# Making twelve weight remainders with an accumulating transfer in place of a VectorE subtraction

## The chip, the cores and the metric

The kernel runs on one core of one Trainium2 chip. The metric is device time in microseconds (us) for one execution, taken as the median of several runs; lower is better. Beside the times there is a profile of one execution: for each engine of the core (TensorE for matrix products, VectorE and ScalarE for work on elements, GpSimd and SyncE, which here mostly issue transfers) when each instruction ran, and for the transfers when they were issued and landed.

## The reference

The reference is a decoder trunk of two layers over 512 tokens of width 1024, in float32. Each layer is a half-step SwiGLU feed-forward, a mixer, and a second half-step SwiGLU. The change is in the mixer, whose first step is one projection of the normalised input:

```python
h = rms_norm(x, mix_norm[l]) @ w_mix_in[l]
(c_x, c_b, c_c, h_q, h_f, h_i, h_g, f_q, f_k, f_v, f_f) = jnp.split(h, split_at, axis=-1)
y = jnp.concatenate([short_conv_mixer(...), hgrn2_mixer(h_q, h_f, h_i, h_g, ...), fox_mixer(...)], axis=-1)
x = x + y @ w_mix_out[l]
```

`h_f`, `h_g` and `h_q` are 256 columns each: the forget logits, the gate and the query of a gated linear recurrence (HGRN2). The products must be close to float32 exact.

## The kernel before

**Products in three parts.** TensorE takes float32 operands at full rate in a rounded form, fp32r. To keep the accuracy, each operand is split in two: `hi`, the value rounded to fp32r, and `lo`, the remainder `src - hi`. A product is then three: hi x hi, hi x lo and lo x hi, all accumulated in one PSUM bank. This is `mm3` (lines 321 to 339); its three matmuls stand in the profile as L328, L336 and L337. Where weights are the first operand, as in the streams below, L328 and L336 read the weight's `hi`, and L337 reads its `lo`.

**Granules.** Weights come from DRAM in granules of two blocks of 128 rows. `granule` (lines 289 to 304) loads one into a tile `st` of 128 partitions by up to 1024 elements (two buffers) on the sync queue (L297), and calls `parted` (lines 306 to 319). That makes a tile `hl` (three buffers) that holds `hi` in its first and `lo` in its second half: a cast on ScalarE (L314), then a subtraction on VectorE (L315). `st` can be loaded again when both have read it; `hl` when the granule's last matmul has read it.

**Streams.** `stream_steps` (lines 345 to 382) walks over the eight blocks of 128 rows (KD = 8) in four granules, k = 0, 2, 4 and 6, and issues their matmuls. For 256 columns there are two jobs, one for each 128 columns with a bank of its own; a granule is 2 blocks x 2 jobs x 3 products = 12 matmuls that move 512 tokens each. The remainder of a granule is first read by its third matmul. The last granule of a stream goes job by job, the others block by block.

**The start of the mixer.** In `mix` (from line 1030) three such streams follow each other: `bz` (forget logits, L1092), `bg` (gate, L1093) and `bq` (query, L1116). They begin while the feed-forward before them ends: its last granules and the norm's sums are still on the engines. Before the last granule of `bz`, `norm` closes the root mean square (L447, and the activations at L277). Then comes a stream with 264 columns that uses tokens as the first operand (L1122), and the recurrence starts. GpSimd's queue holds a memset, a copy and eight small loads of constants at the mixer's beginning (L1043 to L1055); their tiles lie where tiles of the feed-forward were, and so they wait for its last instructions. Between the mixers GpSimd issues the accumulating transfers of the feed-forward (L786, L827).

**What sets the order.** The program is traced in the order of the code. The framework then places each instruction on its engine by readiness in its own estimate and by priority, gives out tile buffers, and adds the semaphores; on the chip every engine runs its own list in order. The work of `parted` stands in a block of high priority when the granule is made ahead, as it is in these three streams. `follow` fixes the order by hand in the feed-forward, not here.

The functions that the diff touches:

Of the kernel before, what the change touches and what calls it, by code (L numbers as in the profile page):

```python
# [9 lines left out]
F32 = mybir.dt.float32  # L10
F32R = mybir.dt.float32r
# [3 lines left out]
AF = mybir.ActivationFunctionType  # L15
ALU = mybir.AluOpType
# [8 lines left out]
P = 128  # L25
# [3 lines left out]
KD = D // P  # L29
# [22 lines left out]
C_X, C_B, C_C, H_Q, H_F, H_I, H_G = (256 * i for i in range(7))  # L52
# [107 lines left out]
class Trunk:  # L160
# [115 lines left out]
    def act(self, out, in_, func, **kw):  # L276
        i = self.nc.scalar.activation(out, in_, func, **kw)  # L277
        if self.tab is not None:
            self.tc.add_manual_dep(i.ins, self.tab, NOSYNC, reason="table order")
        self.tab_users.append(i.ins.name)  # L280
        return i
# [4 lines left out]
        self.chain[engine] = i.ins.name  # L286


    def granule(self, parts, kk, ahead=True, skew=0, keep=False, queued=False, first=False):
        nc = self.nc  # L290
        c = sum(ap.shape[1] for ap in parts)
        st = self.wp.tile([P, 1024], F32, tag="st", name=self.n("st"), bufs=2)
        s3 = st[:, : kk * c].rearrange("p (k c) -> p k c", k=kk)
        at = 0
        for ap in parts:
            w = ap.shape[1]
            d = nc.sync.dma_start(s3[:, :, at : at + w], ap.rearrange("(k p) c -> p k c", p=P))  # L297
            if queued:
                self.follow("s", d)
            at += w  # L300
        with self.tc.high_priority() if ahead and not keep else ExitStack():
            hi, lo = self.parted(st[:, : kk * c], 1 if ahead else kk, skew, keep or first)
        h3, l3 = (a.rearrange("p (k c) -> p k c", k=kk) for a in (hi, lo))
        return [(h3[:, i, :], l3[:, i, :]) for i in range(kk)]

    def parted(self, src, pieces=1, skew=0, keep=False):
        nc = self.nc
        n = src.shape[1]
        hl = self.wp.tile([P, 2 * 1024 + 64], F32R, tag="hl", name=self.n("hl"), bufs=3)
        hh, ll = (hl[:, a + skew : a + skew + n] for a in (0, 1024))  # L310
        w = n // pieces
        for c in range(0, n, w):
            hi, lo = hh[:, c : c + w], ll[:, c : c + w]
            a = nc.scalar.copy(hi, src[:, c : c + w])  # L314
            b = nc.vector.tensor_sub(lo, src[:, c : c + w], hi)  # L315
            if pieces > 1 or keep:
                self.follow("a", a)
                self.follow("v", b)
        return hh, ll
# [22 lines left out]
        for _ in self.stream_steps(*args, **kw):  # L342
            pass

    def stream_steps(self, jobs, parts_of, act, nk, mid=None, pre=None, given=None, queued=False, ending=None, calm=False):
        k = 0
        while k < nk:
            kk = min(2, nk - k)
            if callable(mid) and k == nk - 2:
                mid()  # L350
            if pre is not None:
                pre(k)
            end = k + kk == nk
            if end and ending is not None:
                jobs = ending
            skew = SKEW_MOVING if jobs[0][2] is not None and jobs[-1][0].shape[-1] < T else 0
            keep = given is not None and given(k)
            rows = self.granule(
                parts_of(k, kk), kk, pre is None and not (calm and k == 0), skew, keep,
                queued, queued and k == 0,  # L360
            )
            if keep:
                yield
            order = (
                [(job, j) for job in jobs for j in range(kk)]
                if end
                else [(job, j) for j in range(kk) for job in jobs]
            )
            for n, ((acc, cols, toks, *more), j) in enumerate(order):
                if pre is not None and n == len(order) // 2:  # L370
                    pre(k, True)
                if isinstance(mid, tuple) and (k, len(order) // 2) == (mid[0], n):
                    mid[1]()
                ah, al = act(k + j)
                hi, lo = rows[j]
                first, last = k + j == 0 and not more, end and j == kk - 1
                if toks is None:
                    self.mm3(acc, hi[:, cols], lo[:, cols], ah, al, first, last)
                else:
                    self.mm3(acc, ah[:, toks], al[:, toks], hi[:, cols], lo[:, cols], first, last)  # L380
            k += kk
            yield
# [647 lines left out]
    def mix(self, l, w, w_out, conv_w, out_gain, q_gain, k_gain, f_bias, next_gain):  # L1030
        nc, tc = self.nc, self.tc
        FM2 = [slice(0, P), slice(P, 2 * P)]
        TOK = [slice(c, c + P) for c in (0, 128, 256, 384)]
        with tc.tile_pool(name=self.n("mix"), bufs=1) as mp:
# [23 lines left out]
            def cols(*spans):  # L1058
                return lambda k, kk: [w[k * P : (k + kk) * P, a : a + n] for a, n in spans]

            def features_steps(spans, banks, mid=None):
                bs = [self.bank(t) for t in banks]
                yield from self.stream_steps(
                    [(b, c, None) for b, c in zip(bs, FM2)], cols(*spans), self.xact, KD, mid
                )
                return bs

            def features(*args):
                g = features_steps(*args)
                while True:  # L1070
                    try:
                        next(g)
                    except StopIteration as e:
                        return e.value

            def tokens(a, banks=("mm", "mm")):
# [12 lines left out]
            norm = lambda: self.end_norm(  # L1089
                self.bank("pt"), hp, self.parted_norm(hp, (self.tt,) * 2, self.tb)  # L1090
            )
            bz = features([(H_F, 256)], ("mm", "mm"), norm)  # L1092
            bg = features([(H_G, 256)], ("mm", "po"))  # L1093
            inv = self.inv
            z, q = (hp.tile([P, 2, T], F32, tag=t, name=self.n(t)) for t in ("z", "q"))
            sg = hb.tile([P, 2, T], F32, tag="sg", name=self.n("sg"))
# [16 lines left out]
                out=self.inv2, in0=self.invc, scalar=1.0 / HD, in1=self.invc,  # L1113
                op0=ALU.mult, op1=ALU.mult,
            )
            bq = features([(H_Q, 256)], ("mm", "mm"))  # L1116

            for i in range(2):
                nc.vector.tensor_mul(q[:, i, :], bq[i], inv)
# [64 lines left out]
            def conv():  # L1184
                for i in range(2):
                    bx, bc = yield from features_steps(
                        [(C_X + i * P, P), (C_C + i * P, P)], ("mm", "mm")
                    )
                    if i == 0:
                        inv2 = ap2.tile([P, T], F32, tag="t", name=self.n("iv2"), bufs=self.tb)  # L1190
                        nc.scalar.activation(inv2, inv, AF.Square)
                    self.conv_in(ap2, i, bx, bc, inv2, cw)
                bb = yield from features_steps([(C_B, 256)], ("mm", "mm"))
                for i in range(2):
                    self.conv_out(ap2, i, bb[i])
# [43 lines left out]
            for dg in range(2):  # L1239
                banks = self.next4()  # L1240
# [676 lines left out]
```

## Time and profile before

| | |
|---|---|
| median of 3 runs | 1803.4 us (1801.94 to 1804.28) |
| span of the profiled execution, first to last instruction | 1799.0 us |
| time of the profiled execution itself | not given apart from its span; the runs are 2.9 to 5.3 us above the span |
| TensorE busy | 1791.7 us, 14271 matmuls |
| VectorE busy | 1441.6 us, 2022 instructions |
| ScalarE busy | 993.2 us, 1429 instructions |
| GpSimd busy | 176.9 us, 184 instructions |
| the three streams, first mixer | 336.9 to 370.0 us of the span |
| the three streams, second mixer | about 889.9 us later |

In the lines that follow, a group reads: source line, engine, operation, the tile written and the tiles read, partitions x elements and type, count, then busy time in us and the mean of one in ns, and the idle time of the engine before these instructions with what ended it. In a timeline a line begins with the start and the duration in us. PE is TensorE, DVE is VectorE, ACT is ScalarE, POOL is GpSimd, SP is SyncE; a q behind the name is the engine's queue of issued work. Matmul durations are modelled and overlap; what counts is the distance from one start to the next.

### The profile page before, as it was taken

How to read it: one execution, taken by the hardware profiler on the slowest of the kernel's cores; microseconds unless marked ns; L12 is line 12 of the kernel's file. 1: busy time of each engine (PE TensorE's matmuls, PEld its weight loads, DVE VectorE, ACT ScalarE, POOL GpSimd, SP SyncE). 2: the span in 40 equal slices, each digit the busy share in tenths (PEclk: the TensorE clock that was granted, in tenths of full speed). 3: DMA queues.
4: the chain of work that ended last, by engine and by line, in shares of the span. 5: the costliest groups of instructions: out<-in, count | busy, mean ns of one | idle time of the engine just before them, and what ended most of it. 6: DMA issues, size and time to landing. Idle time of an engine off the chain costs nothing.

```text
span 1799.0 us, 34748 instructions
## 1 busy us (share of the span) xinstructions
PE 1791.7 (100%) x14271; PEld 1681.2 (93%) x14271; DVE 1441.6 (80%) x2022; ACT 993.2 (55%) x1429; POOL 176.9 (10%) x184
## 2 busy tenths in 40 slices
PE   9999999999999999999999999999999999999999
PEld 7899999899888899999889999998998888999997
DVE  9888887776888798879679887876868879888893
ACT  6455554464776464556446555555547755555551
POOL 0011120100000002112001111201000000020210
PEclk9999999999999999999999999999999999999999
DMA  7668783233433857868275787813234346686762
GB/s 209 178 144 184 180 180 96 71 81 84 106 103 104 228 136 160 194 162 165 82 208 132 170 187 187 172 65 83 78 86 115 89 143 180 165 163 189 161 133 94
DMA packets 244638, 254.09 MB, mean 141 GB/s; under 512 B 18904, under 2 KB 228576, under 8 KB 244480
## 3 DMA queue, kind: packets, MB, share of 16 engines
q1 hardware_dynamic: 189424, 182.38, 33.3%
q0 software_dynamic: 54752, 69.23, 23.8%
q8 instruction: 112, 1.84, 0.4%
q14 instruction: 46, 0.38, 0.1%
q10 hardware_dynamic: 304, 0.27, 0.1%
HBM read 223.98 MB, written 2.10 MB: 126 GB/s over the span
## 4 chain that ended last, share of the span: by engine, by line
PE 96%; DVE 2%; ACT 1%; DMA 0%; issue 0%; SPq 0%; ACTq 0%; DVEq 0%
PE mm L328 14%; PE mm L336 14%; PE mm L337 14%; PE sc L328 7%; PE sc L336 7%; PE sc L337 7%; PE pt L328 6%; PE pt L336 6%; PE pt L337 6%; PE po L328 4%; PE po L336 4%; PE po L337 4%; PE po L1648 1%; PE pt L1692 1%; PE sc L1841 1%; PE pt L1841 1%
## 5 line engine op out<-in xcount | busy, mean ns | idle before, releaser
L810 ACT CAST hl<-w 128x1024 fp32r<-128x1024 f32 x322 | 336.9, 1050 | 312.1 <-PE mm L337 82.7
L812 DVE TENSOR_TENSOR hl<-w,hl 128x1024 fp32r<-128x1024 f32 x322 | 392.4, 1222 | 80.4 <-ACT hl L810 80.4
L315 DVE TENSOR_TENSOR hl<-st,hl 128x512 fp32r<-128x512 f32 (+3 forms) x196 | 162.7, 831 | 115.6 <-ACT hl L314 114.5
L314 ACT CAST hl<-st 128x512 fp32r<-128x512 f32 (+3 forms) x196 | 143.1, 732 | 173.7 <-PE po L337 67.8
L328 PE MATMUL mm<-xc,hl 128*128 128x256 f32 (+1 forms) x733 | 201.2, 276 | 0.0
L336 PE MATMUL mm<-xc,hl 128*128 128x256 f32 x728 | 201.2, 276 | 0.0
L337 PE MATMUL mm<-xc,hl 128*128 128x256 f32 x728 | 201.0, 276 | 0.0
L328 PE MATMUL sc<-xc,hl 128*128 128x256 f32 (+1 forms) x532 | 146.0, 276 | 0.0
L336 PE MATMUL sc<-xc,hl 128*128 128x256 f32 x528 | 146.0, 276 | 0.0
L337 PE MATMUL sc<-xc,hl 128*128 128x256 f32 x528 | 145.8, 276 | 0.0
L328 PEld LDWEIGHTS mm<-xc,hl 128*128 128x128 f32 x733 | 137.4, 188 | 0.2
L336 PEld LDWEIGHTS mm<-xc,hl 128*128 128x128 f32 x728 | 136.7, 188 | 0.0
L337 PEld LDWEIGHTS mm<-xc,hl 128*128 128x128 f32 x728 | 136.7, 188 | 0.0
L328 PE MATMUL pt<-xc,hl 128*128 128x256 f32 (+1 forms) x482 | 132.6, 276 | 0.0
L336 PE MATMUL pt<-xc,hl 128*128 128x256 f32 x480 | 132.6, 276 | 0.0
L337 PE MATMUL pt<-xc,hl 128*128 128x256 f32 x480 | 132.5, 276 | 0.0
L328 PE MATMUL mm<-x,hl 128*128 128x512 f32 x272 | 107.6, 396 | 0.0
L336 PE MATMUL mm<-x,hl 128*128 128x512 f32 x272 | 106.3, 391 | 0.0
L337 PE MATMUL mm<-x,hl 128*128 128x512 f32 x272 | 106.2, 390 | 0.0
L328 PEld LDWEIGHTS sc<-xc,hl 128*128 128x128 f32 x532 | 99.7, 188 | 0.2
L336 PEld LDWEIGHTS sc<-xc,hl 128*128 128x128 f32 x528 | 99.1, 188 | 0.0
L337 PEld LDWEIGHTS sc<-xc,hl 128*128 128x128 f32 x528 | 99.1, 188 | 0.0
(512 smaller groups left out, 5579.6 us busy)
## 6 DMA issues: line engine op xcount, KB each, us to landing
w<-in_ffn_w_in_dram SPq DMA_DIRECT2D x140, 512.0 KB, 5.6
w<-in_ffn_w_out_dram SPq DMA_DIRECT2D x64, 512.0 KB, 4.6
w<-in_ffn_w_out_dram POOLq DMA_DIRECT2D x56, 512.0 KB, 8.2
st<-in_w_mix_in_dram SPq DMA_DIRECT2D x88, 256.0 KB, 2.7
st<-in_ffn_w_in_dram SPq DMA_DIRECT2D x70, 256.0 KB, 2.9
w<-in_ffn_w_in_dram POOLq DMA_DIRECT2D x35, 512.0 KB, 8.5
w<-S POOLq DMA_DIRECT2D x35, 512.0 KB, 4.8
st<-in_ffn_w_out_dram SPq DMA_DIRECT2D x24, 512.0 KB, 6.0
```

Of the source, the lines that this page charges most:

```text
L314: a = nc.scalar.copy(hi, src[:, c : c + w])
L315: b = nc.vector.tensor_sub(lo, src[:, c : c + w], hi)
L328: i = nc.tensor.matmul(acc[:, c], ah, bh[:, c], start=first and c.start == 0, stop=False, skip_group_check=True,)
L336: nc.tensor.matmul(acc, a, b, start=False, stop=False, skip_group_check=True)
L337: i = nc.tensor.matmul(acc, c, d, start=False, stop=last, skip_group_check=True)
L810: A(nc.scalar.copy(hi, src))
L812: return lambda: V(nc.vector.tensor_sub(lo, src, hi))
L1648: nc.tensor.matmul(self.ob[:, t0 + u * P : t0 + 2 * P], V[:, j, h % 4].rearrange("p a d -> p (a d)"), part[:, j, u:, :].rearrange("p i t - ...
L1692: nc.tensor.transpose(tb[:, j * P : (j + 1) * P], p[:, j * P : (j + 1) * P], self.ident)
L1841: E(nc.tensor.matmul(acc, wh[j][l][:, cols], (self.xh, self.xl)[r][k + j], start=k + j == 0 and which == 0, stop=k + j == KD - 1 and which ...
```

## The change

For six granules in each mixer, those with k = 2 and k = 6 of the three streams `bz`, `bg` and `bq`, the remainder is made in another way. ScalarE first writes the negated rounded value into `lo`. GpSimd then issues a transfer from `st` to `lo` that adds, which leaves `src - hi` there. ScalarE makes `hi` with a second cast, as before. VectorE has no part in these granules. The other granules, and all other streams, stay as they were.

```diff
-    def granule(self, parts, kk, ahead=True, skew=0, keep=False, queued=False, first=False):
+    def granule(self, parts, kk, ahead=True, skew=0, keep=False, queued=False, first=False, adding=False):
...
         with self.tc.high_priority() if ahead and not keep else ExitStack():
-            hi, lo = self.parted(st[:, : kk * c], 1 if ahead else kk, skew, keep or first)
+            if adding:
+                hi, lo = self.parted_by_transfer(st[:, : kk * c], skew)
+            else:
+                hi, lo = self.parted(st[:, : kk * c], 1 if ahead else kk, skew, keep or first)
...
+    def parted_by_transfer(self, src, skew):
+        nc = self.nc
+        n = src.shape[1]
+        hl = self.wp.tile([P, 2 * 1024 + 64], F32R, tag="hl", name=self.n("hl"), bufs=3)
+        hi, lo = (hl[:, a + skew : a + skew + n] for a in (0, 1024))
+        nc.scalar.activation(lo, src, AF.Copy, scale=-1.0)
+        nc.gpsimd.dma_start(lo.bitcast(F32), src, accum_op=ALU.add)
+        nc.scalar.copy(hi, src)
+        return hi, lo
...
             rows = self.granule(
                 parts_of(k, kk), kk, pre is None and not (calm and k == 0), skew, keep,
-                queued, queued and k == 0,
+                queued, queued and k == 0, k in adding,
             )
...
-            bz = features([(H_F, 256)], ("mm", "mm"), norm)
-            bg = features([(H_G, 256)], ("mm", "po"))
+            bz = features([(H_F, 256)], ("mm", "mm"), norm, (2, 6))
+            bg = features([(H_G, 256)], ("mm", "po"), None, (2, 6))
...
-            bq = features([(H_Q, 256)], ("mm", "mm"))
+            bq = features([(H_Q, 256)], ("mm", "mm"), None, (2, 6))
```

`features` and `features_steps` pass the tuple on to `stream_steps` as `adding`.

More of the change, by code (lines that the diff above doesn't have):

```diff
@@ L343, in stream, with stream_steps @@
             pass
-    def stream_steps(self, jobs, parts_of, act, nk, mid=None, pre=None, given=None, queued=False, ending=None, calm=False):
+    def stream_steps(self, jobs, parts_of, act, nk, mid=None, pre=None, given=None, queued=False, ending=None, calm=False, adding=()):
         k = 0
@@ L1059, in cols, with features_steps @@
                 return lambda k, kk: [w[k * P : (k + kk) * P, a : a + n] for a, n in spans]
-            def features_steps(spans, banks, mid=None):
+            def features_steps(spans, banks, mid=None, adding=()):
                 bs = [self.bank(t) for t in banks]
                 yield from self.stream_steps(
-                    [(b, c, None) for b, c in zip(bs, FM2)], cols(*spans), self.xact, KD, mid
+                    [(b, c, None) for b, c in zip(bs, FM2)], cols(*spans), self.xact, KD, mid,
+                    adding=adding,
                 )
```

## The prediction

> **What bounds the kernel now.** I read the page first: its busy times, then its chain of work that ended last.
>
> ```profile
> PE 1791.7 (100%) x14271; PEld 1681.2 (93%) x14271; DVE 1441.6 (80%) x2022; ACT 993.2 (55%) x1429; POOL 176.9 (10%) x184
> ...
> PE 96%; DVE 2%; ACT 1%; DMA 0%; issue 0%; SPq 0%; ACTq 0%; DVEq 0%
> ```
>
> TensorE is busy 1791.7 of 1799.0 us, so 7.3 us are left to gain in the whole program. Next I read TensorE's waits by what it waited for (us in total, times, longest), whole program; two that belong to its first 5 us are left out:
>
> ```profile
> PE pt L1692 <- DVE QA L1594: 1.3, 2, 0.6
> ...
> PE sc L1625 <- DVE rs L1634: 0.6, 1, 0.6
> PE sc L1625 <- DVE PL L1695: 0.2, 1, 0.2
> ```
>
> None of these lines is in the three streams that the diff touches, and L315, the subtraction it takes away, is no releaser. Number the twelve granules of the three streams G0 to G11: k = 2 and k = 6 of each stream are G1, G3, G5, G7, G9 and G11. Busy time by stretch in the first mixer, from G0's first product to G11's last, the norm's two products left out, and then the next stream:
>
> ```profile
> core 0: us, PE busy (x) PEld busy (x) DVE busy (x) ACT busy (x) POOL busy (x), PEclk, DMA share, GB/s
> 336.88:345.05 8.17, 8.17 (x37) 6.76 (x36) 7.01 (x12) 4.74 (x8) 2.87 (x7) 1.00 0.31 65
> 345.51:356.39 10.88, 10.88 (x50) 9.01 (x48) 8.74 (x15) 5.37 (x8) 2.12 (x3) 1.00 0.39 92
> 356.39:369.99 13.60, 13.60 (x62) 11.27 (x60) 8.02 (x12) 9.19 (x11) 0.00 (x0) 1.00 0.39 99
> 369.99:381.60 11.61, 11.61 (x97) 11.61 (x96) 11.13 (x14) 5.92 (x10) 0.00 (x0) 1.00 0.35 91
> ```
>
> TensorE is full in every one, at full granted clock. Relief of VectorE here has nothing to shorten; the question is whether the longer way to the remainder makes TensorE wait. Its pace is the deadline. Third products (L337, the one that reads the remainder) of G3, G5, G7, G9 and G11:
>
> ```profile
> 345.96 0.39 PE L337 MATMUL mm<-x,hl 128*128 128x512 f32 x1
> ...
> 351.40 0.39 PE L337 MATMUL mm<-x,hl 128*128 128x512 f32 x1
> ...
> 356.84 0.39 PE L337 MATMUL mm<-x,hl 128*128 128x512 f32 x1
> ...
> 362.28 0.39 PE L337 MATMUL mm<-x,hl 128*128 128x512 f32 x1
> ...
> 367.72 0.39 PE L337 MATMUL mm<-x,hl 128*128 128x512 f32 x1
> ```
>
> One granule takes 2.72 us, a pair 5.44. What lets the casts start is seen in ScalarE's timeline (the bracket is its idle time and what ended it):
>
> ```profile
> 331.64 0.62 ACT L314 CAST hl<-st 128x512 fp32r<-128x512 f32 x1 [4.81 <-PE po L337]
> ...
> 340.01 0.60 ACT L314 CAST hl<-st 128x512 fp32r<-128x512 f32 x1
> ...
> 349.10 0.62 ACT L314 CAST hl<-st 128x512 fp32r<-128x512 f32 x1
> 351.15 0.62 ACT L314 CAST hl<-st 128x512 fp32r<-128x512 f32 x1 [1.43 <-PE po L337]
> 353.87 0.62 ACT L314 CAST hl<-st 128x512 fp32r<-128x512 f32 x1 [2.10 <-PE po L337]
> ```
>
> These are G1, G3, G6, G7 and G8. They wait for a product, that is for one of the three hl buffers, not for data: a cast runs two granules (5.44 us) ahead of its use, and that lead is the cover.
>
> **The change, part by part.** Per granule it removes one subtraction on VectorE and adds one cast on ScalarE (groups with shapes kept apart: busy, mean ns):
>
> ```profile
> L315 DVE TENSOR_TENSOR hl<-st,hl 128x512 fp32r<-128x512 f32 x124 | 85.3, 689 | 61.9 <-ACT hl L314 60.8
> ...
> L314 ACT CAST hl<-st 128x512 fp32r<-128x512 f32 x124 | 76.2, 618 | 87.3 <-PE mm L337 39.4 <-PE po L337 37.5 <-DMA st<-in_w_mix_in_dram 6.3
> ```
>
> Twelve in all: 12 x 0.689 = 8.3 us off VectorE, 12 x 0.618 = 7.4 us onto ScalarE. Both lie under TensorE and cost nothing by themselves: over G0 to G11 ScalarE is busy 19.3 of 32.65 us and gets 3.7 more, with the lead of 5.44 as cover. The cast of hi now comes 0.62 later and keeps more than 3 us of that lead.
>
> It adds one accumulating transfer of 256 KB (128 x 512 f32) from st to lo per granule, issued by GpSimd, which this trace does not have at this size. The nearest rows are the 512 KB accumulating transfer SBUF to SBUF and the 128 KB plain ones; of each source line the issue's duration and the time from issue to landing:
>
> ```profile
> L827 POOL DMA_DIRECT2D w<-S x35: 877/887/897, 73.5 to 1729.1; - x35
> ...
> DMA to landing us min/median/max: 4.5/4.8/6.2
> ```
>
> ```profile
> L1599 POOL DMA_DIRECT2D KA<-KA x12: 524/524/545, 473.2 to 1422.8; - x12
> ...
> DMA to landing us min/median/max: 2.1/2.2/2.9
> ```
>
> So L, issue to landing, lies between 2.2 and 4.8. Less the issue, the transfers take 4.8 - 0.89 = 3.9 for 512 KB and 2.2 - 0.52 = 1.7 for 128 KB; on the line between them 256 KB takes 2.4, and with 128 rows to issue (0.89) L = 3.3. I take that, because the new transfer has the rows of the first and a size nearer the second. The Trainium skill, "DMA: Bandwidth & Descriptors", section "Anatomy of one DMA — SWDGE (gpsimd) path", has about 2.0 us fixed plus bytes over 436 GB/s; that would be 2.6 us here by estimate, but for the 512 KB row it gives 3.2 where the trace has 4.8. By the page the slower rival below would cost nothing.
>
> With L = 3.3 the remainder of one granule alone comes 0.62 + 3.3 = 3.9 us after the buffer is free, before 5.44 + 0.45: hidden. What is late next is st. It has two buffers, and its release moves from the subtraction's end to the transfer's landing. Loads of G6, G7, G8 and G10 on the sync queue (each starts when the granule two before it is subtracted), and the time to landing of all loads from 315 to 385 us:
>
> ```profile
> 344.03 0.37 SPq L297 DMA_DIRECT2D st<-in_w_mix_in_dram  x1
> ...
> 347.54 0.37 SPq L297 DMA_DIRECT2D st<-in_w_mix_in_dram  x1
> ...
> 350.48 0.37 SPq L297 DMA_DIRECT2D st<-in_w_mix_in_dram  x1
> ...
> 355.93 0.37 SPq L297 DMA_DIRECT2D st<-in_w_mix_in_dram  x1
> ```
>
> ```profile
> DMA to landing us min/median/max: 2.6/2.7/2.8
> ```
>
> An untouched granule holds st for 2.7 (load) + 0.62 + 0.69 = 4.0 us, a changed one for 2.7 + 0.62 + 3.3 = 6.6. Two buffers give 2 x 5.44 = 10.9 us per pair; 10.6 are asked. It fits if a load takes whichever buffer is free first, and does not if changed granules always get the same one: 6.6 against 5.44. The code leaves that to the framework's list scheduling; the trace before cannot tell, as both rules alternate there.
>
> GpSimd's queue also counts. Around the streams it holds the mixer's constants:
>
> ```profile
> 342.18 0.42 POOL L1043 MEMSET zm<- 128x384 bf16 x1 [66.83 <-DVE sqa L425]
> 342.54 0.29 POOL L1044 COPY zm<-maskb 128x128 bf16<-128x128 bf16 x1
> 342.77 1.12 POOL L1048 DMA_DIRECT2D og<-in_hgrn_out_gain_dram  x2
> ...
> 345.47 2.16 POOL L1054 DMA_DIRECT2D cw<-in_conv_w_dram  x3
> ```
>
> That memset waits until 342.18. G1 and G3 are ready to transfer at about 332.3 and 340.6, before it, so I place them ahead. G5 (loaded from 343.9, cast by 347.3) finds the queue busy to 345.47 + 2.16 = 347.63. Behind the added waits stand: on the sync queue the next granule's load; on ScalarE the norm's Ln and Exp; on GpSimd these constants, of which VectorE waits for one, with the norm's steps behind it:
>
> ```profile
> 346.74 0.14 DVE L1051 TENSOR_SCALAR qkg<-qkg 64x1 f32<-64x1 f32 x1 [2.73 <-DMA qkg<-in_fox_q_gain_dram]
> ```
>
> Should G3's issue, 0.89 long, push that back by as much, to 347.6, the norm's steps and the first reading of the stream's banks still have 11 us until G8 (356.39 + 2.72 = 359.1) wants these banks again. So no cost.
>
> **The sum.** First-free buffers: G6 frees its st at 350.44 (before the load at 350.48), so G7 loads there, casts at 353.2, and its remainder lands at 353.2 + 0.62 + 3.3 = 357.1, 0.3 behind 356.84. G8 frees its own at 355.9, as the load of G10 at 355.93 shows, and G9 takes it: 355.9 + 2.7 + 0.62 + 3.3 = 362.5, on time behind that 0.3. G10 follows G7 at 357.1 and is done at 357.1 + 4.0 = 361.1; G11 takes that buffer: 361.1 + 6.6 = 367.7, on time. An added cast can also meet a table load,
>
> ```profile
> 347.81 1.28 ACT L268 ACT_TABLE_LOAD   x1
> ...
> 361.12 1.28 ACT L268 ACT_TABLE_LOAD   x1
> ```
>
> and I count half of one, 0.6. So 0.9 per mixer, 1.8 for both: span 1799.0 + 1.8 = 1800.8. The page gives no other time of its own execution; the runs' median, 1803.4, is 4.4 above the span, and I keep that: **1805.2**. From L and the table loads this case alone runs from 0 to +3.6: 1803.4 to 1807.0.
>
> **The rivals.**
>
> *Slower: st alternates strictly.* Changed granules then follow one another in one buffer. G5 lands at 347.63 + 3.3 = 350.9; each next one 2.7 + 0.62 + 3.3 = 6.62 later: G7 357.6, G9 364.2, G11 370.8, against 367.72. That is 3.1 per mixer, 6.2 in all: 1809.6. It decides from L = 2.5 on (347.63 + 3 x 3.32 + 4L = 367.72); at L = 4.8 it costs 9.1 per mixer, 1821.6. For it: loads alternate in the rows above. Against it: G6's buffer is free before G5's.
>
> *Slower: a transfer stands behind the constants.* If G3's is queued after the memset and all its loads, it is issued at 347.63 and lands at 350.9, 5.0 behind 345.96; 10 for two mixers, 1813.4. Against it: its cast ends at 340.6, 1.5 us before the memset may start.
>
> *Faster: VectorE's relief reaches the mixer's end.* The waits on QA, rs and PL above sum to 2.1 us, and the chain has 2% of VectorE. Were half of the 8.3 us to shorten it, the time would be 1799.3. Against it: those waits are in the attention (L1594 to L1695), far behind the streams, and VectorE is idle in between (13.60 - 8.02 = 5.6 us in the third stretch).
>
> **How the numbers follow.** Hidden but for crumbs 0.47; strict alternation 0.33; behind the constants 0.10; relief 0.10. A measurement can tell about 0.2%, 3.6 us, from no change: the first case is within it, the next two slower, the last faster. The range leaves out the far end of the second and third cases and the last half of the fourth: 1800.3 to 1811.5.
>
> **What would show it.** Right: VectorE's count 12 lower, ScalarE's 12 higher, twelve new issues of 256 KB on GpSimd landing in 3.0 to 3.6 us, TensorE still full from 336.9 to 370 with loads no longer alternating. Strict alternation shows as TensorE gaps before L337 of G7, G9 and G11, released by a DMA, of about 1 us each. I am wrong if L is far from 3.3, if these gaps sum to over 2 us per mixer, or if TensorE's idle time changes elsewhere.

## The result and the profile after

The changed kernel takes 1812.8 us (median of four runs, 1812.3 to 1814.1) against 1802.8 us for the kernel before on the same chip: ratio 1.0058, interval 1.0046 to 1.0070. It is slower by about 10 us, beyond what the measurement can mistake for nothing, and 1.3 us above the upper end of the predicted range.

The page of the changed kernel, its busy times and the shares of its chain of work that ended last:

```profile
PE 1795.9 (99%) x14271; PEld 1682.3 (93%) x14271; DVE 1434.1 (79%) x2010; ACT 998.7 (55%) x1441; POOL 188.0 (10%) x196
...
PE 91%; DMA 4%; DVE 2%; ACT 2%; issue 1%; SPq 0%; POOL 0%; ACTq 0%; DVEq 0%; POOLq 0%
```

VectorE has 12 instructions fewer, ScalarE 12 more and GpSimd 12 more, as the diff says. The chain has changed its nature: before, 96% of it was TensorE and 0% transfers; now TensorE has 91% and transfers 4%. The span is 1811.3 us, 12.3 more than before. TensorE's waits by what it waited for (us in total, times, longest):

```profile
PE mm L350 <- DMA hl<-st: 6.9, 6, 1.6
...
PE mm L341 <- ACT v L1143: 1.1, 2, 0.6
```

Both lines are new. L350 is the matmul that reads the remainder (L337 before the lines moved). L341 is the first of the three products, and it waits there for a bank that holds v, the result of the stream with 264 columns (here called the fourth stream). Busy time by stretch in the first mixer, for the same matmuls as in the last three of the four stretches shown of before:

```profile
347.36:359.13 11.77, 11.19 (x49) 8.93 (x48) 7.19 (x12) 6.45 (x10) 3.88 (x5) 1.00 0.49 112
359.13:376.42 17.29, 14.20 (x62) 11.11 (x61) 6.68 (x11) 9.74 (x12) 1.70 (x2) 1.00 0.58 124
376.42:388.03 11.61, 11.61 (x98) 11.61 (x97) 10.46 (x14) 5.27 (x9) 0.00 (x0) 1.00 0.40 96
```

Where TensorE was full in 10.88 and 13.60 us, it now idles 0.58 and 3.09 us; the fourth stream itself, the last of these stretches, is as long as before. The granted clock is 1.00 in all three. The places are the third products of G5, G7 and G9. TensorE's timeline, with those of G3 and G11 for comparison:

```profile
347.81 0.39 PE L350 MATMUL mm<-x,hl 128*128 128x512 f32 x1
...
354.00 0.50 PE L350 MATMUL mm<-x,hl 128*128 128x512 f32 x1 [0.58 <-DMA hl<-st]
...
361.24 0.50 PE L350 MATMUL mm<-x,hl 128*128 128x512 f32 x1 [1.49 <-DMA hl<-st]
...
368.58 0.50 PE L350 MATMUL mm<-x,hl 128*128 128x512 f32 x1 [1.60 <-DMA hl<-st]
...
374.15 0.39 PE L350 MATMUL mm<-x,hl 128*128 128x512 f32 x1
```

Set against the same products of before (345.96, 351.40, 356.84, 362.28, 367.72), they come 1.85, 2.60, 4.40, 6.30 and 6.43 us later. The 1.85 us at G3 owe nothing to the change: 1.96 of lateness was there at 32 us of the span already, long before the first changed instruction. TensorE's first 32 us differ by 0 to 2 us between the profiled executions of the kernels below. So the three streams of this mixer lost 6.43 - 1.85 = 4.6 us. The stream behind the fourth loses another 0.8, where it waits for a bank of v (a matmul at 382.29 before runs at 389.49, 7.20 later). That makes 7.20 - 1.85 = 5.35 us for the first mixer. In the second, the third product of G3 is 6.83 us late (1235.86 before, 1242.69 after) and the matmul that waits for v 12.04 (1272.19, 1284.23): 5.2. Some 0.6 us is made good between the mixers, so about 10 us are left, as in the medians.

What each of these products waited for is read from three queues. GpSimd's issues of the transfers of G3, G5, G7 and G9:

```profile
342.77 0.86 POOL L315 DMA_DIRECT2D hl<-st  x1 [7.49 <-DVE x L422]
...
350.58 0.94 POOL L315 DMA_DIRECT2D hl<-st  x1 [1.16 <-ACT hl L314]
357.86 0.89 POOL L315 DMA_DIRECT2D hl<-st  x1 [6.34 <-ACT hl L314]
365.04 0.85 POOL L315 DMA_DIRECT2D hl<-st  x1 [6.30 <-ACT hl L314]
```

The sync queue's loads, ScalarE's negated casts of G5 and G9, and VectorE's subtractions of the untouched G6, G8 and G10, which free the other `st` buffer:

```profile
346.24 0.88 SPq L297 DMA_DIRECT2D st<-in_w_mix_in_dram  x2
354.01 0.88 SPq L297 DMA_DIRECT2D st<-in_w_mix_in_dram  x2
361.24 0.88 SPq L297 DMA_DIRECT2D st<-in_w_mix_in_dram  x2
366.53 0.37 SPq L297 DMA_DIRECT2D st<-in_w_mix_in_dram  x1
```

```profile
349.65 0.63 ACT L314 ACTIVATE hl<-st 128x512 fp32r<-128x512 f32 x1 [1.40 <-DMA st<-in_w_mix_in_dram]
...
364.11 0.63 ACT L314 ACTIVATE hl<-st 128x512 fp32r<-128x512 f32 x1 [5.53 <-DMA st<-in_w_mix_in_dram]
```

```profile
352.62 0.68 DVE L328 TENSOR_TENSOR hl<-st,hl 128x512 fp32r<-128x512 f32 x1
...
358.62 0.69 DVE L328 TENSOR_TENSOR hl<-st,hl 128x512 fp32r<-128x512 f32 x1
...
365.81 0.69 DVE L328 TENSOR_TENSOR hl<-st,hl 128x512 fp32r<-128x512 f32 x1 [1.28 <-ACT hl L327]
```

Last, the time from issue to landing of the transfers of this mixer:

```profile
DMA to landing us min/median/max: 3.3/3.4/3.5
```

Read in turn, these are one ring. The transfer of G5 is issued at 350.58 and lands 3.4 us later, at 354.0; at 354.01 the next two loads start. The transfer of G7 is issued at 357.86 and lands at 361.2; at 361.24 the next two loads start. The first of them, G9's, goes into the buffer that the transfer just left: the other one was free from 358.62 + 0.69 = 359.31 on, and no load started then. ScalarE waits for that load until 364.11, casts for 0.63, and 0.30 later, at 365.04, the transfer of G9 is issued. So a changed granule follows the changed one before it at 365.04 - 357.86 = 7.2 us, where TensorE needs one every 5.44. ScalarE is no longer released by a product, as in the rows of before, but by a load. The loads come in twos because the sync queue is a list in order: the other buffer is free, but its load (G10's, at 361.70) stands behind one that waits for a transfer.

### The profile page after: what moved, and what is told of

It reads as the page before. It is cut to its first block, busy times and chain, and to the rows that moved or that the text cites. A ratio compares the mean times of both kernels' runs of the same rounds, so it can differ in the third digit from the quotient of the medians.

```text
span 1811.3 us, 34767 instructions
## 1 busy us (share of the span) xinstructions
PE 1795.9 (99%) x14271; PEld 1682.3 (93%) x14271; DVE 1434.1 (79%) x2010; ACT 998.7 (55%) x1441; POOL 188.0 (10%) x196
## 4 chain that ended last, share of the span: by engine, by line
PE 91%; DMA 4%; DVE 2%; ACT 2%; issue 1%; SPq 0%; POOL 0%; ACTq 0%; DVEq 0%; POOLq 0%
PE mm L341 13%; PE mm L349 13%; PE mm L350 13%; PE sc L341 6%; PE sc L349 6%; PE sc L350 6%; PE pt L341 6%; PE pt L349 6%; PE pt L350 6%; PE po L349 3%; PE po L341 3%; PE po L350 3%; DMA st<-in_w_mix_in_dram 2%; DMA hl<-st 1%; PE po L1662 1%
## 5 line engine op out<-in xcount | busy, mean ns | idle before, releaser
L328 DVE TENSOR_TENSOR hl<-st,hl 128x512 fp32r<-128x512 f32 (+2 forms) x184 | 154.2, 839 | 100.5 <-ACT hl L327 99.4
L327 ACT CAST hl<-st 128x512 fp32r<-128x512 f32 (+2 forms) x184 | 135.6, 739 | 140.8 <-PE po L350 40.8
L341 PE MATMUL mm<-xc,hl 128*128 128x256 f32 (+1 forms) x733 | 201.3, 276 | 0.0
L350 PE MATMUL mm<-xc,hl 128*128 128x256 f32 x728 | 201.0, 276 | 0.0
L341 PE MATMUL sc<-xc,hl 128*128 128x256 f32 (+1 forms) x532 | 146.0, 276 | 0.0
L350 PE MATMUL sc<-xc,hl 128*128 128x256 f32 x528 | 145.8, 276 | 0.0
L341 PEld LDWEIGHTS mm<-xc,hl 128*128 128x128 f32 x733 | 137.4, 188 | 0.2
L350 PEld LDWEIGHTS mm<-xc,hl 128*128 128x128 f32 x728 | 136.7, 188 | 0.0
L341 PE MATMUL pt<-xc,hl 128*128 128x256 f32 (+1 forms) x482 | 132.6, 276 | 0.0
L350 PE MATMUL pt<-xc,hl 128*128 128x256 f32 x480 | 132.5, 276 | 0.0
L350 PE MATMUL mm<-x,hl 128*128 128x512 f32 x272 | 107.0, 393 | 7.0 <-DMA hl<-st 6.9
L341 PE MATMUL mm<-x,hl 128*128 128x512 f32 x272 | 107.7, 396 | 0.0
L341 PEld LDWEIGHTS sc<-xc,hl 128*128 128x128 f32 x532 | 99.7, 188 | 0.2
L350 PEld LDWEIGHTS sc<-xc,hl 128*128 128x128 f32 x528 | 99.1, 188 | 0.0
```

Source lines behind the costliest of these rows:

```text
L341: i = nc.tensor.matmul(acc[:, c], ah, bh[:, c], start=first and c.start == 0, stop=False, skip_group_check=True,)
L350: i = nc.tensor.matmul(acc, c, d, start=False, stop=last, skip_group_check=True)
```

## The experiments

Theories at the start. **A**: the transfer holds `st` until it lands, the next granule in that buffer is loaded late, and this is the loss. **B**: the transfer is simply too long for the lead of two granules, whatever the buffer. **C**: ScalarE's added casts delay its list. After the first runs A was refined to **A1** (untouched granules catch up what was lost), and **D** was set against it: each changed granule costs 0.8 to 0.9 us of its own, wherever it stands. All edits are against the changed kernel.

### Buffers of their own, and the casts alone

In the first, G5, G7, G9 and G11 are loaded into two buffers that the mixer has lying idle at that time. In the second ScalarE keeps its negated cast, but VectorE writes the remainder over it as before.

```diff
+        self.granules = 0
...
-        st = self.wp.tile([P, 1024], F32, tag="st", name=self.n("st"), bufs=2)
+        if adding and self.granules > 4:
+            st = self.mp.tile([P, 4, 4, 2, HD], F32, tag="qk", name=self.n("sa"), bufs=2)
+            st = st.rearrange("p i h w d -> p (i h w d)")
+        else:
+            st = self.wp.tile([P, 1024], F32, tag="st", name=self.n("st"), bufs=2)
+        self.granules += 1
```

> The changed granules from the second stream on (G5, G7, G9, G11 of each mixer) load into two buffers of their own; all else as in the changed kernel. Theory A (the transfer holds st past its landing, 3.4 us from issue, and the next changed granule's load waits for the same buffer): the waits of TensorE on the transfer go, and the time comes back to 1803 to 1805 us. Theory B (the transfer is too long for the lead of two granules, whatever buffer it reads): still about 1813. Theory C (the added casts delay ScalarE): still about 1813.

```diff
-        nc.gpsimd.dma_start(lo.bitcast(F32), src, accum_op=ALU.add)
         nc.scalar.copy(hi, src)
+        nc.vector.tensor_sub(lo, src, hi)
```

> The negated cast and the second cast stay on ScalarE for the twelve granules, but VectorE makes the remainder as before and overwrites the negated value; no transfer. Theory C (ScalarE's 12 added casts cost the time): about 1813. Theories A and B: 1803, as before.

Measured: with buffers of their own 1802.3 us, ratio 1.0000 (0.9991 to 1.0009); with the casts alone 1801.6 us, 0.9996 (0.9987 to 1.0005). Neither has a wait of TensorE in the streams among its listed waits; with own buffers two short pauses at the third products of G3 and G5 cost 0.8 us in the first mixer and nothing in the second. With their own buffers the transfers of G7, G9 and G11 are 5.9 and 5.8 us apart, close to TensorE's pace, instead of 7.2; the last two go out on GpSimd at

```profile
359.42 0.85 POOL L321 DMA_DIRECT2D hl<-sa  x1 [4.98 <-ACT hl L320]
365.24 0.85 POOL L321 DMA_DIRECT2D hl<-sa  x1 [4.97 <-ACT hl L320]
```

The whole loss goes with the shared buffer, although each of these transfers takes longer than in the changed kernel (median 3.9 us to landing, against 3.4). So B falls, and C falls with the second kernel. It also shows what the relief of VectorE is worth: all subtractions of the changed granules are still gone in the first kernel, and nothing is won.

### Other granules, and fewer

Three edits of the tuples only: k = 2 and 4 instead of 2 and 6; k = 2 alone in each stream; and the pair left out of the query stream.

```diff
-            bz = features([(H_F, 256)], ("mm", "mm"), norm, (2, 6))
-            bg = features([(H_G, 256)], ("mm", "po"), None, (2, 6))
-            bq = features([(H_Q, 256)], ("mm", "mm"), None, (2, 6))
+            bz = features([(H_F, 256)], ("mm", "mm"), norm, (2, 4))
+            bg = features([(H_G, 256)], ("mm", "po"), None, (2, 4))
+            bq = features([(H_Q, 256)], ("mm", "mm"), None, (2, 4))
```

> As many changed granules, but k = 2 and k = 4 of each stream in place of k = 2 and k = 6: G1, G2, G5, G6, G9, G10. Each st buffer then alternates a changed granule (about 7.2 us held: load 2.9, cast 0.63, hop 0.3, transfer 3.4) with an untouched one (about 4.3), 11.5 us for two granules against 10.9 that TensorE gives. Theory A: 0.3 to 0.8 us lost per mixer, 1803.5 to 1804.5 us. Theories B and C: as many transfers and casts, still about 1813.

```diff
+            bz = features([(H_F, 256)], ("mm", "mm"), norm, (2,))
+            bg = features([(H_G, 256)], ("mm", "po"), None, (2,))
+            bq = features([(H_Q, 256)], ("mm", "mm"), None, (2,))
```

> Only k = 2 of each stream is changed: G1, G5, G9, all in the same st buffer, with untouched granules between. Theory A: held 7.2 + 4.3 = 11.5 us per two uses, no transfer late: 1802 to 1804 us. Theories B and C: half the changed granules, half the loss, about 1808.

```diff
-            bq = features([(H_Q, 256)], ("mm", "mm"), None, (2, 6))
+            bq = features([(H_Q, 256)], ("mm", "mm"))
```

> Changed granules k = 2 and k = 6 in the first two streams only (G1, G3, G5, G7), none in the third. Theory A1 (the transfer holds st, loads fall behind from G5 on, and what is late at the end of the third stream is handed on to the fourth): 0.6 us at G5 and 1.8 us at G7 as in the changed kernel, and the untouched third stream catches up: 2.4 per mixer, about 1807.5. Theory D (each changed granule costs the same, 0.8 to 0.9 us, wherever it stands): 8 of them, about 1809.

Measured: 1812.4 us (ratio 1.0061, 1.0049 to 1.0074), 1807.1 us (1.0024, 1.0014 to 1.0033) and 1809.7 us (1.0045, 1.0032 to 1.0058). A missed all three numbers: it said that a distance of four granules, or untouched granules after the changed ones, would give the time back. The numbers that B and C gave for the first two (about 1813 and 1808) came closer, and so did D's for the third (1809), although B and C had fallen. TensorE's waits in the second and the third of these kernels:

```profile
PE mm L341 <- DVE q L1133: 2.4, 2, 1.4
...
PE mm L341 <- ACT v L1143: 1.1, 2, 0.5
```

```profile
PE mm L350 <- DMA hl<-st: 4.0, 4, 1.6
PE mm L341 <- DVE q L1133: 1.3, 2, 0.9
```

With only k = 2 changed there is no wait for a transfer at all, and yet TensorE loses, now for the read-outs of q and v: the one of q frees a bank for the fourth stream, the one of v a bank for the stream behind it. So the lateness was not made good; it moved.

### Two granules, and one

```diff
-            bz = features([(H_F, 256)], ("mm", "mm"), norm, (2, 6))
-            bg = features([(H_G, 256)], ("mm", "po"), None, (2, 6))
-            bq = features([(H_Q, 256)], ("mm", "mm"), None, (2, 6))
+            bz = features([(H_F, 256)], ("mm", "mm"), norm, (2,))
+            bg = features([(H_G, 256)], ("mm", "po"), None, (2,))
+            bq = features([(H_Q, 256)], ("mm", "mm"))
```

> Only k = 2 of the first two streams is changed: G1 and G5. Theory A1: G5's transfer holds one load back, and the six untouched granules after it catch up: 0 to 0.5 per mixer, 1802 to 1803.5. Theory D: 4 changed granules, about 1806.

The next one changes only G9, k = 2 of the query stream.

> Only k = 2 of the third stream is changed: G9, one granule per mixer. Theory A1: the loss of the run with k = 2 in all three streams came at the fourth stream, from loads behind G9's transfer and VectorE's list behind their subtractions, so most of it stays: 1.5 to 2.5 per mixer, 1805.5 to 1807.5. Theory D: 2 changed granules, about 1804.

Measured: 1806.1 us (1.0022, 1.0013 to 1.0031) with G1 and G5, and 1803.2 us (1.0009, 1.0000 to 1.0019) with G9 alone. D's numbers fit better again: over these kernels 1, 2, 3, 4 and 6 changed granules per mixer cost 1.2, 4.1, 4.7, 7.8 and 10 us. But D names no mechanism. The kernel with G1 and G5 has the start of before (no shift of TensorE until 371.09), so its rows stand beside those of before directly. Its waits:

```profile
PE mm L341 <- DVE q L1133: 1.4, 2, 0.9
...
PE mm L341 <- ACT v L1143: 1.1, 2, 0.6
```

VectorE and ScalarE before, with ScalarE's cast of G10 first:

```profile
359.31 0.62 ACT L314 CAST hl<-st 128x512 fp32r<-128x512 f32 x1 [2.10 <-PE po L337]
```

```profile
368.66 0.71 DVE L315 TENSOR_TENSOR hl<-st,hl 128x528 fp32r<-128x528 f32 x1 [0.39 <-ACT hl L314]
369.28 0.69 DVE L1119 TENSOR_TENSOR q<-mm,inv 128x512 f32<-128x512 f32 x1
```

```profile
380.55 1.06 ACT L277 ACTIVATE T<-T 128x1024 f32<-128x1024 f32 x1 [0.88 <-DVE T L1326]
381.51 0.46 ACT L1129 ACTIVATE v<-mm,invc 128x264 f32<-128x264 f32 x1
```

and with G1 and G5 changed:

```profile
361.15 0.62 ACT L327 CAST hl<-st 128x512 fp32r<-128x512 f32 x1 [2.95 <-DMA st<-in_w_mix_in_dram]
```

```profile
370.47 0.71 DVE L328 TENSOR_TENSOR hl<-st,hl 128x528 fp32r<-128x528 f32 x1 [0.58 <-ACT hl L327]
371.10 0.68 DVE L1133 TENSOR_TENSOR q<-mm,inv 128x512 f32<-128x512 f32 x1
```

```profile
382.36 1.06 ACT L277 ACTIVATE T<-T 128x1024 f32<-128x1024 f32 x1 [0.76 <-DVE T L1340]
383.33 0.46 ACT L1143 ACTIVATE v<-mm,invc 128x264 f32<-128x264 f32 x1
```

The order is the same, all of it 1.8 us later. The subtraction at 370.47 belongs to an untouched granule of the fourth stream, its second (G13), eight granules behind the last changed one. Both `st` buffers have been handed on late ever since G5: G10's cast waits for its load (361.15), where before it waited for a product. In ScalarE's list the gate's activation and the recurrence's exponentials stand behind that cast, and G13's cast behind those; it starts at 369.80, 0.07 us after the exponential ahead of it ends. The read-out of q stands behind G13's subtraction in VectorE's list, and everything of the recurrence behind that; the read-out of v stands behind the recurrence's exponential in ScalarE's list. The matmuls that stood at 371.09 and 382.29 before come 0.75 us and then another 0.8 later for want of these banks. With 1.8 us at the same two places of the second mixer that is 3.4 of the 4.1 us.

### The order of VectorE's list

If this reading is right, part of the loss goes when only the order is changed. The same two granules, with the fourth stream's subtractions from its second granule on put behind the first read-out of q:

```diff
+            if self.behind is not None:
+                self.tc.add_manual_dep(b.ins, self.behind, NOSYNC, reason="given order")
...
-            for i in range(2):
-                nc.vector.tensor_mul(q[:, i, :], bq[i], inv)
+            reads = [nc.vector.tensor_mul(q[:, i, :], bq[i], inv) for i in range(2)]
...
-            self.stream(
+            for k in self.stream_steps(
                 [(bv[i][:, :264], slice(0, 264), TOK[i]) for i in range(4)],
                 cols((H_I, 256), (F_F, 8)), self.xact, KD,
-            )
+            ):
+                self.behind = reads[0].ins.name
+            self.behind = None
```

> The kernel that changes only the granules G1 and G5 (1806.1 us), with one order given: VectorE's subtractions for the fourth stream from its second granule on stand behind the first read-out of q. VectorE's list then has the order of the two variants that lose nothing: q ahead of the subtraction, and the recurrence's T ahead of z times q. Theory A with hand-on by the list: the load that is late after G5 no longer holds the read-outs, the two TensorE waits of 0.75 and 0.8 us per mixer go; 1802 to 1803.5 us. Theory D (a changed granule costs 0.8 us wherever and however the lists stand): 1805.5 to 1806.5 us.

Measured: 1803.7 us, 1.0013 (1.0004 to 1.0022). That is 0.2 above A's range, but more than half of the 4.1 us is gone with as many granules changed, which speaks against a fixed cost per granule (D). The two intervals overlap; that the order did it is seen in the waits. The one for q is gone, the one for v is not:

```profile
PE mm L344 <- ACT v L1147: 1.3, 2, 0.8
```

In ScalarE's list the cast of a late granule still stands ahead of the gate's activation and of the recurrence's exponentials behind that:

```profile
361.89 0.62 ACT L328 CAST hl<-st 128x512 fp32r<-128x512 f32 x1 [3.03 <-DMA st<-in_w_mix_in_dram]
362.41 1.05 ACT L278 ACTIVATE sg<-sg 128x1024 f32<-128x1024 f32 x1
```

In the kernel with the casts alone the same cast waits for a product, not for a load:

```profile
360.36 0.62 ACT L327 CAST hl<-st 128x512 fp32r<-128x512 f32 x1 [1.58 <-PE po L350]
```

So the lateness is handed on by two lists, and the edit mended one. Two variants that lose nothing (own buffers, casts alone) also have q ahead of that subtraction in their lists, given so by the framework's own scheduling. That made the order a rival explanation for them. But the changed kernel, which loses 10 us, has this order too:

```profile
375.25 0.69 DVE L1133 TENSOR_TENSOR q<-mm,inv 128x512 f32<-128x512 f32 x1 [0.37 <-PE mm L350]
...
378.37 0.71 DVE L328 TENSOR_TENSOR hl<-st,hl 128x528 fp32r<-128x528 f32 x1 [1.13 <-ACT hl L327]
```

So that order alone does not save the time. The next three runs test the buffer itself.

### The held buffer alone

First, the transfer made longer with the buffers as they are: two halves, one behind the other.

```diff
-        nc.gpsimd.dma_start(lo.bitcast(F32), src, accum_op=ALU.add)
+        for c in range(0, n, n // 2):
+            nc.gpsimd.dma_start(
+                lo[:, c : c + n // 2].bitcast(F32), src[:, c : c + n // 2], accum_op=ALU.add
+            )
```

> The changed kernel with each remainder's transfer issued as two transfers of 128 KB, one behind the other on GpSimd's queue. The second issue comes some 0.86 us after the first, so the pair lands an estimated 0.5 to 0.9 us later than the 3.4 us of one. Theory A (the transfer holds the granule's st buffer, and the next granule in that buffer waits): every microsecond that the pair lands later is added to the cycle load, negated cast, transfer, four times per mixer: 4 x 0.7 x 2 = 5.6 us more than the changed kernel, 1816 to 1820 us. Theory D (each changed granule costs 0.8 to 0.9 us of its own, however long the transfer): 1812 to 1814 us. A theory by which the list order on VectorE is the cause says the same as D.

Second, the transfer does not read `st`, but the weights in DRAM (`ap`, the granule's part of them, is passed on):

```diff
...
-        nc.gpsimd.dma_start(lo.bitcast(F32), src, accum_op=ALU.add)
+        nc.gpsimd.dma_start(
+            lo.rearrange("p (k c) -> p k c", k=2),
+            ap.rearrange("(k p) c -> p k c", p=P), accum_op=ALU.add,
+        )
```

> The changed kernel with the accumulating transfer reading the weights a second time from DRAM instead of from the st buffer; the two st buffers and their turns stay. The buffer is then free after ScalarE's two casts, but the remainder comes no sooner: an estimated 3.3 to 4.5 us after the negated cast, since the loads from DRAM take 2.7 to 3.4 us in these traces. Theory A: the waits for hl<-st in the gate streams go, TensorE waits at most where the remainder itself is late; 1801 to 1805 us. Theory D, and the theory that the order of VectorE's list is the cause: 1810 to 1814 us as in the changed kernel.

Third, the longer transfer and buffers of its own, that is both edits together:

> Both edits together: G5, G7, G9 and G11 load into two buffers of their own, and each transfer is issued in two halves, 0.5 to 0.9 us longer. In the kernel with the buffers of its own the transfers of G7, G9 and G11 are issued at 353.55, 359.42 and 365.24 us and no TensorE wait names them. Theory A (only the held buffer costs): 1802 to 1804 us, since nothing waits for the buffer and the remainder has time to spare. Theory B (the remainder itself comes too late for a lead of two granules once the transfer is a little longer): 0.5 to 0.9 us for each of three granules per mixer, 1805 to 1808 us.

Measured: 1817.2 us (1.0087, 1.0072 to 1.0101), 1806.0 us (1.0026, 1.0016 to 1.0036) and 1802.4 us (1.0003, 0.9994 to 1.0012). With halves the issues of G5 and G7 are

```profile
350.38 1.84 POOL L316 DMA_DIRECT2D hl<-st  x2 [0.96 <-ACT hl L314]
358.04 1.72 POOL L316 DMA_DIRECT2D hl<-st  x2 [5.82 <-ACT hl L314]
```

7.7 us apart instead of 7.3, and from G7 to G9 it is 7.6 instead of 7.2. The same longer transfer costs 5 us more where it holds `st`, and nothing where the granules have buffers of their own. So it is the hold, and the remainder's own lead has room to spare. D is out: kernels that all change six granules per mixer lose 15 us (halves), 10 (one transfer), 4 (from DRAM) and 0.5 (halves, own buffers). The 5 us came as A's number said, but not all as A said it: the ring grew by only 0.4 us, not 0.7, the waits for the transfer grew by 1.5 us over both mixers, and the rest is new waits behind them:

```profile
PE mm L353 <- DMA hl<-st: 8.4, 8, 2.3
PE mm L352 <- DVE hl L331: 2.2, 2, 1.2
```

Reading from DRAM took away the ring (no wait at G7 and G9) and 6 of the 10 us. It is 1 us above A's range. What is left are waits at G5 and G11 for a longer transfer:

```profile
PE mm L353 <- DMA hl<-in_w_mix_in_dram: 2.4, 3, 1.2
```

```profile
hl<-in_w_mix_in_dram POOLq DMA_DIRECT2D x6, 256.0 KB, 4.7
```

```profile
346.29 2.24 POOL L1070 DMA_DIRECT2D cw<-in_conv_w_dram  x3
348.41 1.37 POOL L315 DMA_DIRECT2D hl<-in_w_mix_in_dram  x1
```

G5's negated cast ends at 346.8, but its transfer is issued at 348.41, behind the constants, and it takes 4.7 us. So the rival "behind the constants" has a part in it, for G5 rather than G3; the other part is the longer transfer, and no run separates the two. Together they cost 0.8 us in this mixer.

### The sync queue's order

The loads that come in twos suggested one more cause: the load that waits for a transfer blocks the next one. With k = 2 alone, the loads of k = 6 were issued by GpSimd instead (`load` is GpSimd for these granules). The diff is against the kernel with k = 2 alone:

```diff
...
-            d = nc.sync.dma_start(s3[:, :, at : at + w], ap.rearrange("(k p) c -> p k c", p=P))
+            d = (load or nc.sync).dma_start(s3[:, :, at : at + w], ap.rearrange("(k p) c -> p k c", p=P))
```

> k = 2 of all three streams changed, as in the run that measured 1807.1, and the loads of the k = 6 granules of these streams, which reuse the buffer that a transfer holds, are issued by GpSimd in place of the sync queue. If the cost comes from the untouched loads that stand behind them on the sync queue (G8, G12): below half of the loss remains, 1803 to 1804.5. If it comes from the buffer itself: 1807 or, as a load issued by GpSimd takes longer, more.

Measured: 1810.6 us (1.0054, 1.0041 to 1.0067), 3.5 us more than the same granules with all loads on the sync queue.

```profile
PE mm L341 <- DVE q L1133: 4.2, 2, 2.6
```

The lateness grew at the read-outs of q, and waits for the transfer came back (1.6 us). Whether the sync queue's order costs anything by itself stays open: the loads that GpSimd issued also took longer, 3.7 us to landing (median) against 2.8 for the loads of the kernel with k = 2 alone.

## Why the prediction was wrong

**What bounds the kernel: right.** VectorE's relief was said to have nothing to shorten. In the kernel with buffers of their own the relief is whole and the time is that of before.

**The casts at no cost: right.** The kernel with the casts alone is at 0.9996. The 0.6 us per mixer for a table load in the way were not needed.

**L = 3.3: right.** It is 3.4. Here the Trainium skill, "DMA: Bandwidth & Descriptors", section "Anatomy of one DMA — SWDGE (gpsimd) path", gave 2.6 by estimate; the trace does not agree. With that 2.6 the prediction's sum for strict alternation would have come to 0.3 us per mixer (347.63 + 3 x 3.32 + 4 x 2.6 = 368.0, against 367.72). Taking L from the two rows of the trace was the better choice.

**The step that failed** is this one: "It fits if a load takes whichever buffer is free first, and does not if changed granules always get the same one". The first was taken, with 0.47. The trace of after shows the second for G5, G7 and G9: every landing is followed at once by a load, and that load's granule is the next to be cast, transferred and waited for. A load does not take the buffer that is free first: the one of G6 was free at 353.30 and the one of G8 at 359.31, and the loads of G7 and G9 started at 354.01 and 361.24. So the sum's 6.6 us had to fit into 5.44, not two holds into 10.9, and the ring measures 7.2. Only G11 got out of it: its load starts at 366.53, right behind G10's subtraction (365.81 + 0.69 = 366.50) and before the third landing, and in this mixer no listed wait stands at its product. The prediction's evidence against alternation ("G6's buffer is free before G5's") used the load of G6 as it was before, at 344.03. In the changed kernel that load stands behind G5's on the sync queue, and G5's waits for G3's landing at 346.2, so G6 is late as well. The step took the times of one granule's load from the trace before although the change moves them.

**The rival with the right mechanism was priced too low**: 3.1 us per mixer against 5.35 in the first. Three terms were too small or missing.

- The ring was put at 2.7 + 0.62 + 3.3 = 6.62 us; it measures 7.2. Of the difference 0.30 is the hop from ScalarE's cast to GpSimd's issue, which the sum didn't have; the load to the cast took 2.9 instead of 2.7; the transfer 3.4.
- It began later: G5's transfer was put at 347.63, or 349.5 with this execution's shift of 1.85. It went out at 350.58: the constants were past by then (they end at 349.42), but from its load to G5's cast 3.4 us went by instead of 2.7 (346.24 to 349.65). Why is not shown; two loads started at once there, but so they did for G7 and G9, with 2.9. So up to G9 6.30 - 1.85 = 4.45 us were lost where the sum had 364.2 - 362.28 = 1.9. The last step of the sum, G11's, did not come.
- Nothing was counted behind the streams. The wait for v adds 0.8 per mixer; the runs with fewer granules show that this is lateness handed on through the `st` buffers and two lists.

**Behind the constants: right for G3.** Its transfer (342.77) is ahead of the memset (343.31). It is G5's that meets them in the kernel that reads from DRAM.

**The range** stopped at 1811.5 because it cut the far end of the alternation rival, whose bounds were those of L alone. L was as taken; the terms that were off had no bounds at all.

**What it had named as a sign** came: gaps before the third product of G7 and G9 (and of G5) released by a DMA, together 3.7 us in the first mixer where over 2 were named.

## What to carry to other kernels

When work moves from an engine to a transfer, ask what the transfer reads and for how long that cannot be reused. The transfer's result may be early enough and the buffer it reads still be the bound. Work out the ring (load, cast, hop, transfer, load) for the buffer that the changed steps share, start it from loads that the change itself has moved, and set it against the consumer's pace. A pipeline that is full has little slack to catch up with (here 0.6 us between the mixers): what is late once is handed on through the buffers and the engines' lists to the next place with none to spare, so look there too.

## What the runs showed of the hardware

- An accumulating transfer of 256 KB takes 3.4 us from issue to landing when it reads SBUF (median of the changed kernel; 3.9 in the kernel with buffers of their own), and 4.8 when it reads DRAM (4.7 in the first mixer). In two halves each takes 3.0 (median), and the pair makes the ring only 0.4 us longer.
- From the end of ScalarE's cast to GpSimd's issue 0.30 us pass (364.11 + 0.63 = 364.74, issue at 365.04).
- Two loads of 256 KB issued together on one queue let the first cast start after 3.4 us (346.24 to 349.65) in one case and 2.9 in two others; alone they landed in 2.6 to 2.8 in the kernel before.
- TensorE's first 32 us differ by 0 to 2 us between the profiled executions of kernels whose code is the same there, so spans of single profiles can mislead by as much.
